# New places for the pieces of a hand-woven schedule: first layer's input, attention, delta layer

## The chip, the cores and the metric

The kernel runs on one core of one Trainium2 chip. The metric is the device time of one execution in microseconds (us), median of several runs. Of the kernel before, three runs are known: 3433.69, 3437.28 and 3441.73 us.

## The reference, cut to what matters

Two layers over x [2048, 1024]. Layer 0 is sparse attention on a latent, layer 1 a gated delta rule; after each comes a gated embedding. In the shape that the kernel uses:

```python
h = rms_norm(x, norm_w[0])
c_q, c_kv, k_idx, w_idx, z = split(h @ a_w_in)            # latents, each normed
score = sum_h relu(q_idx_h @ k_idx.T) * w_idx_h           # choose 256 keys per query
o = softmax(q_lat @ c_kv.T + bias, on the chosen keys) @ c_kv
x = x + ((o @ w_uv) * silu(z)) @ a_w_out;  x = x + sigmoid(...) * (p[0] @ ple_w_proj[0])

q, k, v = silu(causal_conv(h2 @ b_w_in));  beta, g = ...  # per head, in chunks
lower = strict(beta * k @ k.T * decay);   T = inverse(I + lower)
for each chunk:                                           # state S [128, 128] per head
    u = T @ (v - exp(g) * k @ S);  o = exp(g) * q @ S + (q @ k.T * decay) @ u
    S = S * decay_end + k_dec.T @ u
x = x + (rms_norm(o) * silu(z)) @ b_w_out;  x = x + sigmoid(...) * (p[1] @ ple_w_proj[1])
```

## The kernel before, in words

Every large matmul is done on values split into a high and a low part, as three matmuls (`mm3_step`, L90 to L92). TensorE therefore has most of the work, and the other engines prepare operands and take results out of PSUM.

The order of the work is written by hand. Each stage is a set of Python generators, the streams; a stream yields a position before each of its pieces, and `weave` always runs the piece with the smallest position (of equal ones, that of the stream named first). The order in which pieces are run is their order of priority on every engine and queue; the Tile framework then issues, at each engine, the first piece in that order that its own timing model has as ready. A position is a fraction of its stage (or a cost count), not a time.

The stages, in order of time:

- **Latents** (0 to 190 us). Four blocks of 512 rows. `latents(sb)` runs 22 steps of six matmuls: two column chunks of c_q (`ncq`), one of the index keys (`nki`), two of c_kv (`nkv`), with `at()` giving step n the position n / 23.7367. Beside it `enter(sb + 1)` loads the four 128-row tiles of the next block (`load_x`: a 512 KB load, a square with row sum on ScalarE into a scratch tile, a scale on VectorE), transposes and splits them into `hT`. The square of each chunk (`ncq..sq`, L265 to L268) and the scratch of `load_x` (`xsq`, L182) share the tag `sq`, which has two buffers. The sums over rows of the squares are matmuls with a column of ones (L276). `keep` writes the split input to HBM, two 512 KB writes at each of four steps.
- **Scores** (190 to 838 us). `index` (scores of the indexer), `topk` (bisection on VectorE and ScalarE), and `rest` (the gates z, keys, values, queries). `PLAN` gives index and topk of each block its window in units; 518 units is the whole.
- **Attention** (838 to 1414 us). `logits`, values (`turn` transposes the probabilities, `mult` multiplies with the values two turns later, at a place set by `MP`), loads, and at the start `proj_v`. `cost`, `C0` and `DELTA` say how far the values run behind the logits; `VS`, `VL`, `V0` place what comes before the first logits.
- **First mix**, then the **delta layer** (about 1840 to 3080 us), then the second mix. The delta layer has 18 passes j, each a weave. `project(j)` projects head j: tensors k, q, z, v in this order, two halves each, 32 steps of six 512-column matmuls (pieces `pB`). `within(j-1)` and `beside(j-1)` prepare the head before: k transposed (`pkt`), products (`pkk`, `pkq`), the inverse of a triangular matrix by 16 steps on VectorE (`tmp`, `inv`, L1639 and L1642), then through HBM (`iv_d`, `Uc`), a transpose `Tc`, and four rounds of small matmuls (`px`, `pd`) that fill `U`. `across(j-2)` carries the state over 8 chunks c of the head before that, each a chain of three pieces: `pks` (k and q times the state), `pu` (U times `y`), `po` (gives the new state). `gated` ends a head. `ahead` takes the place of project in the last two passes: first blocks of the output projection (`poe`).

Between the three pieces of a chunk stand small instructions of other engines: `pks` is followed by VectorE's `y` (L1749), `pu` by ScalarE's `uu` (L1757), `po` by VectorE's `state` (L1762). `raw_weights` splits the next tensor's weights: a copy on ScalarE (L1317) and a subtraction on VectorE (L1319, `wB`), each made to follow the last instruction that across has put on that engine.

```python
t0 = AC + c * AD                  # AC, AD = 0.0, 0.11
yield t0                          # pks, then y on VectorE
yield t0 + 0.035                  # pu, then uu on ScalarE
yield t0 + 0.07                   # po, then state on VectorE
```

## Time and profile before

| what | value |
|---|---|
| median of 3 runs | 3437.28 us |
| lowest, highest | 3433.69, 3441.73 us |
| the profiled execution, its time | 3443.02 us |
| its span, first to last instruction | 3441.3 us |
| mean granted TensorE clock in it | 0.982 |
| TensorE busy | 3304.1 us (96%) |
| VectorE, ScalarE, GpSimd busy | 2090.1, 1862.2, 950.1 us |

The profile counts TensorE's matmuls as pipelined, so a busy share is not a share of the peak. PEclk is the granted clock: 1.00 is 2.4 GHz and 0.5 is 1.2 GHz, and a stretch between has part of it at either level. In a timeline row the bracket gives how long the engine stood idle just before the instruction, and what ended the wait.

### The profile page before, as it was taken

To read this page: it belongs to the slowest core of one execution; us is meant where nothing else is said; L and a number is where in the kernel's file an instruction comes from. 1 tells how busy PE (TensorE), PEld (TensorE's weight loads), DVE (VectorE), ACT (ScalarE), POOL (GpSimd) and SP (SyncE) were. 2 spreads that over 40 slices of the span, in tenths; PEclk is the share of its full clock that TensorE was granted. 3 is DMA by queue.
4 is the path that set the end of the run, shared out by engine and by line. 5 is a ranking of instruction groups with operands and counts; after the bars stand their busy time and mean duration, and the time that the engine had idled before them with its cause. 6 is when DMAs were issued, how large, how long until landed. Compare 5 with 4: busy or idle time off the path is not lost.

```text
span 3441.3 us, 51940 instructions
## 1 busy us (share of the span) xinstructions
PE 3304.1 (96%) x18954; PEld 2773.9 (81%) x18954; DVE 2090.1 (61%) x4502; ACT 1862.2 (54%) x3255; POOL 950.1 (28%) x1620
## 2 busy tenths in 40 slices
PE   8999989998899999999999999999999999899999
PEld 6778877887799999888887788887788888678887
DVE  5347996773688888522134577677577677733222
ACT  5356958664677777533335465555565556434221
POOL 2022535246454445211100221231121232321100
PEclk9999999999999999999999999999999999999999
DMA  7532465443422222422222222222222222243212
GB/s 244 178 112 70 128 209 164 168 155 120 152 79 84 79 76 78 159 73 72 66 81 79 51 50 56 53 59 81 62 50 56 53 59 50 86 133 115 74 35 71
DMA packets 327596, 328.46 MB, mean 95 GB/s; under 512 B 69704, under 2 KB 273064, under 8 KB 323240
## 3 DMA queue, kind: packets, MB, share of 16 engines
q1 hardware_dynamic: 327336, 325.11, 31.1%
q8 instruction: 149, 2.44, 0.3%
q14 instruction: 111, 0.91, 0.1%
HBM read 221.24 MB, written 103.81 MB: 94 GB/s over the span
## 4 chain that ended last, share of the span: by engine, by line
PE 54%; DVE 11%; DMA 4%; POOL 2%; ACT 2%; issue 2%; SPq 0%; DVEq 0%; ACTq 0%; POOLq 0%
PE pgm L91 3%; PE pgm L92 3%; PE pgm L90 3%; PE pt L1024 3%; DVE tmp L1639 2%; PE pom L90 2%; PE pom L92 2%; PE pom L91 2%; PE pBv L1521 2%; PE po L1044 2%; PE pBv L1522 2%; PE po L1045 2%; PE lg L92 2%; PE pBv L1523 2%; PE lg L90 2%
## 5 line engine op out<-in xcount | busy, mean ns | idle before, releaser
L79 DVE TENSOR_TENSOR pl<-pt,ph 128x512 fp32r<-128x512 f32 (+1 forms) x288 | 187.7, 658 | 47.3 <-ACT ph L78 45.1
L78 ACT ACTIVATE ph<-pt 128x512 fp32r<-128x512 f32 (+1 forms) x288 | 159.8, 564 | 97.7 <-PE pt L1024 89.0
L1006 ACT ACTIVATE pr<-pr,nm,qscale 128x1024 f32<-128x1024 f32 (+2 forms) x192 | 189.5, 988 | 40.7 <-DVE nm L1003 39.7
L1247 DVE TENSOR_TENSOR gm<-ppm,gm 128x512 f32<-128x512 f32 x64 | 43.4, 690 | 244.3 <-ACT gm L1246 244.3
L423 DVE SCALAR_TENSOR_TENSOR score<-rl,wi,score 128x1024 f32<-128x1024 f32 (+7 forms) x154 | 170.0, 1127 | 35.2 <-ACT rl L415 34.3
L415 ACT ACTIVATE rl<-il 128x1024 f32<-128x1024 f32 (+7 forms) x176 | 142.7, 817 | 74.8 <-PE il L92 69.0
L1024 PE MATMUL pt<-ident,pr 128*128 128x128 f32 x1088 | 169.7, 276 | 8.2 <-ACT pr L1006 5.5
L90 PE MATMUL pom<-wo,ym 128*128 128x512 f32 x432 | 171.1, 396 | 1.9 <-DVE y L1056 1.1
L91 PE MATMUL pom<-wo,ym 128*128 128x512 f32 x432 | 169.4, 392 | 1.3 <-POOL wo L87 1.3
L91 PE MATMUL pgm<-wm,xh 128*128 128x512 f32 x432 | 168.9, 391 | 1.6 <-DVE wm L82 1.6
L729 DVE TENSOR_SCALAR_CACHE_REDUCE tkj<-score,t 128x1664 bf16<-128x1664 f32 (+3 forms) x91 | 121.9, 1353 | 79.0 <-POOL t L769 69.9
L90 PE MATMUL pgm<-wm,xh 128*128 128x512 f32 x432 | 169.0, 391 | 0.7 <-ACT gm L1246 0.6
L92 PE MATMUL pom<-wo,ym 128*128 128x512 f32 x432 | 169.2, 392 | 0.0
L92 PE MATMUL pgm<-wm,xl 128*128 128x512 f32 x432 | 169.0, 391 | 0.0
L1044 PE MATMUL po<-pl,kv 128*128 128x256 f32 x576 | 163.2, 283 | 1.7 <-DVE pl L79 1.6
L1045 PE MATMUL po<-ph,kv 128*128 128x256 f32 x576 | 162.3, 282 | 0.0
L1043 PE MATMUL po<-ph,kv 128*128 128x256 f32 x576 | 161.4, 280 | 0.8 <-ACT ph L78 0.6
L87 POOL TENSOR_TENSOR ym<-yr,ym 128x1024 fp32r<-128x1024 f32 x32 | 77.1, 2409 | 304.7 <-ACT ym L86 304.5
L1246 ACT ACTIVATE gm<-pgm,rm_r 128x512 f32<-128x512 f32 x64 | 42.9, 684 | 183.7 <-PE pgm L91 117.4
L727 ACT ACTIVATE tkj<-score,t 128x1920 bf16<-128x1920 f32 (+3 forms) x91 | 127.8, 1405 | 26.7 <-POOL t L769 13.6
L1752 ACT ACTIVATE qs<-pks,eg 128x128 f32<-128x128 f32 x120 | 44.0, 366 | 179.6 <-DVE y L1749 173.6
L90 PE MATMUL lg<-kv,q 128*128 128x512 f32 (+2 forms) x320 | 139.7, 437 | 0.7 <-DVE mx L997 0.7
(636 smaller groups left out, 10814.6 us busy)
## 6 DMA issues: line engine op xcount, KB each, us to landing
wBr<-in_b_w_in_dram SPq DMA_DIRECT2D x64, 512.0 KB
wr<-in_a_w_in_dram SPq DMA_DIRECT2D x74, 256.0 KB
hT_d<-hT SPq DMA_DIRECT2D x32, 512.0 KB
hz<-hT_d SPq DMA_DIRECT2D x16, 1024.0 KB
yr<-yT_d SPq DMA_DIRECT2D x32, 512.0 KB
x<-in_x_dram SPq DMA_DIRECT2D x16, 512.0 KB
zT_d<-z SPq DMA_DIRECT2D x32, 256.0 KB
k_d<-k SPq DMA_DIRECT2D x16, 512.0 KB
```

What stands on the lines that cost most here:

```text
L78: nc.scalar.activation(hi, src, AF.Copy)
L79: nc.vector.tensor_tensor(lo, src, f32(hi), ALU.subtract)
L90: nc.tensor.matmul(dst, ah, bh, start=first, stop=False)
L91: nc.tensor.matmul(dst, ah, bl, start=False, stop=False)
L92: nc.tensor.matmul(dst, al, bh, start=False, stop=last)
L415: nc.scalar.activation(rl[:, :s1 - s0], pl[:, :s1 - s0], AF.Relu)
L423: nc.vector.scalar_tensor_tensor(sc[:, s0:s1], rl[:, :s1 - s0], w, sc[:, s0:s1], ALU.mult, ALU.add)
L1006: nc.scalar.activation(pr[:, s0:s1], pr[:, s0:s1], AF.Exp, bias=nm, scale=sc, accum_out=den[:, i % 2, x:x + 1])
L1024: nc.tensor.transpose(pt[:, x * P:(x + 1) * P], probs[h, i][:, j * P:(j + 1) * P], ident)
L1043: nc.tensor.matmul(d, V[0][:, j], ph[:, c], start=st, stop=False)
L1044: nc.tensor.matmul(d, V[0][:, j], pl[:, c], start=False, stop=False)
L1045: nc.tensor.matmul(d, V[1][:, j], ph[:, c], start=False, stop=sp)
```

## The change

Positions and constants of the schedule are changed; no instruction is added, removed or changed. Lines without a sign are left out.

```diff
 # enter, latents: input of the first layer
-                yield (i / 8 + b / 4) * 0.989 + 0.0
+                yield (i / 8 + b / 4) * 0.9492 + 0.0812
-            if n in (6, 9, 12, 15):
-                keep(sb, (6, 9, 12, 15).index(n))
-            return n / 23.7367
+            if n in (2, 12, 14, 20):
+                keep(sb, (2, 12, 14, 20).index(n))
+            return n / 22.9662
 # proj_q
-                yield at + 0.013
+                yield at + 0.0181
 # attention
-    C0, DELTA = 1.5, 7.0
+    C0, DELTA = 1.269, 8.2959
-        cost = [4.0 * g + 3 + C0 for _, g in order]
+        cost = [3.7993 * g + 3 + C0 for _, g in order]
-            yield -VS + VL * 0.52
+            yield -VS + VL * 0.6127
-                yield begin[max(n - 2, 0)] + -0.02
+                yield begin[max(n - 2, 0)] + -1.0534
-    MP = 0.9
+    MP = 1.3291
-    VS, VL, V0, V1 = (40.0, 39.5, 39.0, 20)
-    PLAN = ({3: (0, 120), 2: (120, 256), 1: (300, 400), 0: (430, 470)}, {3: (122, 300), 2: (302, 415), 1: (417, 481), 0: (482, 530)}, 518)
+    VS, VL, V0, V1 = (40.0, 39.3825, 38.628, 20)
+    PLAN = ({3: (0, 120), 2: (120, 256), 1: (294, 400), 0: (418, 470)}, {3: (122, 300), 2: (302, 415), 1: (417, 483), 0: (482, 534)}, 518)
 # delta layer: places of within, beside, across, gated, ahead
-    VT, RA, RB = 0.36, 0.31, 0.0127
-    AC, AD, LV = 0.0, 0.11, 0.75
-    FX = 0.02
+    VT, RA, RB = 0.3282, 0.31, 0.0127
+    AC, AD, LV = 0.0, 0.11, 0.8179
+    FX = 0.0104
-                            if (sb, k) == (0, 0):
+                            if (sb, k) == (0, 3):
                                 made["raw"] = load_weights(n + 1)
-                            if (sb, k) == (1, 0):
+                            if (sb, k) == (0, 7):
                                 ready[n + 1] = raw_weights(n + 1, made.pop("raw"))
-            yield from by4(f"pkt{j}", transposes(kT), k_sink, 0.0)
+            yield from by4(f"pkt{j}", transposes(kT), k_sink, 0.0, 0.0297)
-            yield from by4(f"pkk{j}", prod(kT, kT), l_sink, 0.06)
+            yield from by4(f"pkk{j}", prod(kT, kT), l_sink, 0.06, 0.0105)
-            yield RA - 0.04
+            yield RA - 0.0591
-            yield LV - 0.02
+            yield LV - 0.0263
-                yield LV + 0.06 + p * 0.02
+                yield LV + 0.0609 + p * 0.02
-            yield LV + 0.14
+            yield LV + 0.123
-            yield LV + 0.2
+            yield LV + 0.2043
-            yield 0.12
+            yield 0.086
-                t0 = AC + c * AD
+                t0 = AC + c * AD + (c == NC - 1) * -0.0317
-                yield t0 + 0.035
+                yield t0 + 0.0265 + (0.0243 if c > 1 else 0)
-                yield t0 + 0.07
+                yield t0 + 0.0918 + {3: 0.0085, 7: 0.0071}.get(c, 0)
-            yield from by4(f"pot{j}", transposes(o), o_sink, at + 0.05)
+            yield from by4(f"pot{j}", transposes(o), o_sink, at + 0.0469)
-                at = 0.5 + x * 0.25 if part == 0 else x / n
+                at = 0.5842 + x * 0.25 if part == 0 else x / n
-                            yield at + (c * 4 + k // 2 + 1) / 9 * (0.25 if part == 0 else 1.0 / n)
+                            yield at + (c * 4 + k // 2 + 1) / 9 * (0.25 if part == 0 else 1.3319 / n)
```

## Rows read from the trace of the kernel before

**Rows 1.** The page's part 1: busy us, share of the span and instructions.
```profile
PE 3304.1 (96%) x18954; PEld 2773.9 (81%) x18954; DVE 2090.1 (61%) x4502; ACT 1862.2 (54%) x3255; POOL 950.1 (28%) x1620
```
**Rows 2.** Busy time by stage: stretch and length, engines, PEclk, DMA share, GB/s.
```profile
0.00:190.00 190.00, 170.28 (x840) 133.05 (x840) 85.98 (x135) 77.02 (x156) 32.43 (x52) 0.97 0.57 197
190.00:838.00 648.00, 608.69 (x2918) 502.20 (x2919) 492.00 (x704) 438.55 (x691) 258.75 (x554) 0.97 0.43 141
...
900.00:1400.00 500.00, 497.52 (x3639) 465.74 (x3637) 435.41 (x1385) 365.27 (x689) 230.07 (x282) 1.00 0.27 81
...
2480.00:2955.00 475.00, 466.44 (x3124) 388.77 (x3124) 335.50 (x762) 269.01 (x515) 114.59 (x261) 1.00 0.22 54
```
**Rows 3.** TensorE's waits by line, whole span: us in total, times, longest.
```profile
PE pu L1755 <- DVE y L1749: 17.4, 17, 5.4
...
PE ncq2ss L276 <- DVE ncq2sq L268: 3.3, 1, 3.3
PE ncq0ss L276 <- DVE ncq0sq L268: 2.6, 1, 2.6
...
PE px L1664 <- DVE Tc L1652: 2.6, 1, 2.6
```
**Rows 4.** Timelines of VectorE and TensorE in the latents: start, us, instruction, [idle].
```profile
125.15 0.69 DVE L267 TENSOR_TENSOR ncq2sq<-ncq2cr 128x512 f32<-128x512 f32 x1 [4.47 <-ACT xsq L182]
...
126.79 1.84 PE L276 MATMUL ncq2ss<-ones,ncq2sq 128*128 128x1 f32 x8 [3.34 <-DVE ncq2sq L268]
...
164.58 1.02 PE L276 MATMUL ncq3ss<-ones,ncq3sq 128*128 128x1 f32 x8
```
**Rows 5.** Busy time in four short stretches: engines, PEclk, DMA share, GB/s.
```profile
36.00:42.00 6.00, 4.94 (x20) 4.15 (x21) 1.70 (x3) 0.78 (x2) 1.65 (x2) 0.72 0.82 314
120.00:134.00 14.00, 10.10 (x44) 8.55 (x42) 6.82 (x11) 4.01 (x8) 1.95 (x1) 0.76 0.22 79
...
1938.00:1958.00 20.00, 20.00 (x123) 14.43 (x121) 4.31 (x6) 4.64 (x9) 1.15 (x5) 0.57 0.14 28
2672.00:2684.00 12.00, 12.00 (x144) 9.30 (x144) 4.88 (x9) 6.00 (x12) 3.12 (x7) 1.00 0.21 45
```
**Rows 6.** Timeline of TensorE, delta layer's second pass: the first px.
```profile
1937.59 0.66 PE L1664 MATMUL px<-Tc,LT 32*32 32x32 f32 x16 [2.57 <-DVE Tc L1652]
```
**Rows 7.** Timeline of TensorE, one later pass: its first pks, its px, the next pass.
```profile
2613.80 0.38 PE L1747 MATMUL pks<-state,kT 128*128 128x128 f32 x2
...
2672.84 1.09 PE L1664 MATMUL px<-Tc,LT 32*32 32x32 f32 x32
...
2683.18 0.38 PE L1747 MATMUL pks<-state,kT 128*128 128x128 f32 x2
```
**Rows 8.** Timelines of VectorE and TensorE in that pass, around chunk 6.
```profile
2660.54 1.23 DVE L1319 TENSOR_TENSOR wB<-wBr,wB 128x1024 fp32r<-128x1024 f32 x1
2661.68 1.01 DVE L1639 TENSOR_TENSOR tmp<-inv,blk 128x480 f32<-128x480 f32 x1
2662.59 0.35 DVE L1749 SCALAR_TENSOR_TENSOR y<-pks,neg,vt 128x128 f32<-128x128 f32 x1
...
2663.00 0.49 PE L1755 MATMUL pu<-y,U 128*128 128x128 f32 x2 [0.83 <-DVE y L1749]
```
**Rows 9.** Timeline of TensorE, pass without projection: po, then the next chunk's pks.
```profile
2964.15 0.39 PE L1761 MATMUL po<-uu,aq 128*128 128x128 f32 x2
2965.31 0.49 PE L1747 MATMUL pks<-state,kT 128*128 128x128 f32 x2 [0.77 <-DVE state L1762]
```
**Rows 10.** Timelines of VectorE and TensorE at the end of the scores.
```profile
823.20 0.85 DVE L806 TENSOR_TENSOR flags<-got,want 128x2 f32<-128x2 f32 x1
...
837.60 1.87 PE L477 MATMUL psq<-ones,qg 128*128 128x1 f32 x8 [3.06 <-DVE qg L509]
```
**Rows 11.** ScalarE by line, delta layer: count | busy us, mean ns | idle before.
```profile
L1468 ACT ACT_TABLE_LOAD x34 | 43.6, 1283 | 0.6
L1588 ACT ACT_TABLE_LOAD x16 | 20.5, 1283 | 1.2
```

## The prediction, made before the result was known

> **What bounds the kernel now.** I read the page's totals first, then busy time by stage, then TensorE's waits by line, and last the timelines around the longest of them. TensorE is busy for 3304.1 of 3441.3 us [rows 1], so no edit of places can give more than the other 137 us and what the clock gives back after a stall. The stages say where these are: the latents leave TensorE idle 20 of 190 us and the scores 39 of 648, while attention leaves 2.5 of 500 and the delta layer's second half 8.6 of 475 [rows 2]. In the waits the reader should see four that the moved pieces touch: `pu` on VectorE's `y`, 17.4 us, the row sums `ncq..ss` on their squares, 3.3 and 2.6 us, and `px` on `Tc`, 2.6 us [rows 3]. A stall costs twice: in the stretches that hold two of the latents' stalls the granted clock is 0.72 and 0.76, and in the 20 us after the `px` stall it is 0.57, though TensorE is busy through all of them; the same small matmuls of a later pass, with no stall ahead, run at 1.00 [rows 5].
>
> **The change part by part.** A place is a priority. What moves is which piece stands ahead of which, so I merge the streams' positions and count what changes sides.
>
> Latents. A step is 1/23.74 before and 1/22.97 after. `enter`'s piece that loads the last tile stood at 0.247, ahead of step 6; it now stands at 0.319, behind step 7. The second c_q chunk ends with step 7, so its square now comes ahead of that tile's square. Before, it came behind, and the two share a two-buffer scratch whose other buffer the first chunk holds: in the third block the square on VectorE waited 4.47 us for ScalarE's `xsq`, and the row sums stood 3.34 us for it [rows 4]. The fourth block has no next tile, and its row sums have no wait [rows 4]. The edit takes the cause away: 3.3 + 2.6 = 5.9 us of stall [rows 3], and of clock 6 × 0.28 + 14 × 0.24 = 5.1 us [rows 5], 11.0 in all. From the other side: the first of the four `keep` steps, 1 MB of writes, now stands ahead of the third tile's load, and if that tile becomes the late one the three waits come back, 0, or grow by one such stall each, +3 × 3.3 = 10 us. The third tile's square is now due six steps of six matmuls before the second chunk's, which is time enough, so I take 10 of the 11. The other `keep` steps only write to HBM, and the reader (the gates) starts after the stage; cover: the 190 us of the stage, and if a write were late, the next block's split would wait on `hT`, whose two buffers give it a whole block. `enter`'s last transposes stay ahead of step 21, so the next block does not start later.
>
> Scores. Two index windows start 6 and 12 units earlier and two topk windows end 2 and 4 later; a unit is 648/518 = 1.25 us. The last topk then ends 5 us later, at about 828 instead of 823.2, and the last queries end at 837.6 [rows 10]: hidden by some 9 us, and a loss of the excess if that cover went. Queue: the index pieces that move pass gates and value pieces, whose writes stand on SP; nothing else is passed. TensorE can win or lose a wait there, and the nearest row is 3.06 us [rows 10]. I take 0, with ±3. `proj_q`'s place moves inside its own stream, so nothing is passed.
>
> Attention. `VS`, `VL`, `V0` keep all four loads between the same pieces of `proj_v`, so 0. The values run 8.3 units behind the next group's start instead of 7, of some 18 units a group; TensorE idles 2.5 us in 500 [rows 2], so a gain ends there, and a lost wait is bounded by the same 3.06 us. The near bias is prepared about one unit earlier on GpSimd, with its loads on SP, while TensorE has other work. I take 0.
>
> Delta layer, second pass (the first with `within`). `LV` moves `px` from project's step 24 to step 27, and the matmuls behind it as far or somewhat less. Three steps are 18 matmuls; a step lasts about 69.4/32 = 2.2 us in a full pass [rows 7] and less in this one, so `px` comes 4 us or more later, and the 2.57 us that it waited for `Tc` [rows 6] are covered by projection. With the stall goes the low clock after it, 20 × 0.43 = 8.6 us [rows 5]. I take 2.6 + 8.6 = 11; the other end is 0, if the clock falls anyway.
>
> Delta layer, later passes. There `px` already stands 2672.84 - 2613.80 = 59 us into a pass of 69.4 [rows 7], behind where step 27 puts it, so `LV` gives nothing. The waits for `y` are 17.4 us in 17 times, one of them 5.4 in the pass without projection, which leaves 12.0 us for 16 [rows 3]. In a full pass it is chunk 6: `y` stood behind `wB` of 1.23 and a `tmp` of 1.01 us, and `pu` waited 0.83 [rows 8]. The weights' split moves up one matmul step in emission, but it is tied behind across's last instruction, and this is now chunk 5's `y` instead of its `state`, so `wB` goes some microseconds ahead and leaves the gap; the `tmp` stays. `pu` of chunk 6 keeps one step behind its `pks`. One of two obstacles goes: I take half, 6 of 12. The ends: 12 gained, or a loss that the next part prices. The 3-step later load of the weights waits on SP behind nothing new; the split needs it only four matmul steps on, and if it lands late ScalarE stands, with PSUM's two `pa` buffers as cover.
>
> The rest of the delta layer (`beside`, `gated`, the halves of `pkt` and `pkk`, `FX`, `ahead`) crosses a step here and there, beside a TensorE that has projection to do; 0, ±4 as in one such wait of 5.4 us.
>
> Sum: 10 + 11 + 6 = 27 us off the profiled execution's 3443.0, which gives 3416; that execution lies 5.7 us above the median, so against runs it is **3410 us**.
>
> A rule that speaks against the first term: the Trainium skill, Perfetto Trace Analysis (Identifying Performance Opportunities, Optimization Strategy), takes a gap that repeats on the busy engine as a possible sign of too few buffers. By that rule an order alone leaves the latents' stalls, and the sum is 17 us; the trace half agrees, since the wait is for a shared buffer [rows 4].
>
> **The rivals.**
>
> A, in part: one of the two stalls stays, because the third tile, behind 1 MB of writes, takes the last one's part, or because ScalarE or the clock keeps the second pass as it was. For it: both cures rest on one trace. Price: 10 or 11 of 27 us, so 3421.
>
> B, no change: the pieces come out where they stood. For it: `px` stands far behind its written place already [rows 7]. Against it: the latents' wait follows the order of two allocations. Time 3437.
>
> C, slower: the state's update is laid bare. Merging the places, `po` to the next `pks` has no projection step left at chunks 4 to 5 and 6 to 7, and one instead of two elsewhere. Where it is bare, `pks` waited 0.77 us for `state` [rows 9], and with half of a `wB` in flight on VectorE [rows 8] 0.77 + 0.62 = 1.4. Two places in 14 full passes are 28 waits, 39 us; less the 21 of the two stalls, 18 slower: 3455. It decides from 21/28 = 0.75 us a wait. Against it: a `pks` that is not ready lets projection pass.
>
> D, slower in another way: moved squares, exponentials and gates alternate more on ScalarE. There are 34 + 16 table loads at two lines alone, 1283 ns each [rows 11], in 16 heads. Two more a head between `pu` and `uu` are 16 × 2 × 1.28 = 41 us, less 27: 3451. The Trainium skill, ScalarE: Activation LUTs (Table sets: the hidden batching unit), says that each change to a function of another set costs a load, so order decides their number. ScalarE is busy 54% [rows 1], which speaks against.
>
> **How the numbers follow.** Forecast 0.55, A 0.17, B 0.14, C 0.10, D 0.04. A measurement of this kernel tells 0.2%, 7 us, from no change. Faster: forecast and A, 0.72. Same: B, 0.14. Slower: C and D, 0.14. The range's low end takes all gains, 11 + 11.2 + 12 and 3 + 2.5 + 4 from the parts held at 0, 44 us, with 3 for the spread of the runs: 3390. The high end takes in A and B with the upper bound of the runs known, 3442; C and D lie outside.
>
> **What would show it.** Right: no `xsq` ahead of `ncq..sq` and no wait of row sums above 1 us in the first 190 us; the second pass's `px` without a wait and PEclk at 1.00 behind it; fewer or shorter waits of `pu` for `y`. Wrong: waits of `pks` for `state` in every pass, more table loads, waits of row sums as before with a third tile's `xsq`, or a last topk behind the last queries.

## The result, and the profile after

| what | before | after |
|---|---|---|
| median of 6 runs each | 3439.74 us | 3396.76 us |
| lowest, highest | 3433.69, 3442.03 | 3390.05, 3406.71 |
| the profiled execution, its time | 3443.02 | 3399.54 |
| TensorE idle in the span | 137 us | 109 us |

The ratio is 0.9863, with an interval of 0.9844 to 0.9882: 43 us off medians, 43.9 us off the two profiled spans. The page's totals of the changed kernel, against [rows 1]:

```profile
PE 3288.3 (97%) x18954; PEld 2769.2 (82%) x18954; DVE 2113.0 (62%) x4502; ACT 1858.9 (55%) x3255; POOL 946.3 (28%) x1620
```

The counts of instructions are the same. TensorE is idle for 28 us less and busy for 15.8 us less. Summed over the span the latter is not the clock: its mean is 0.982 in both executions. A matmul behind a stall takes longer, as `pks` in two timelines below, 0.49 us with a wait and 0.38 without.

Where it went is read from the starts of five groups of matmuls: the last `pwi` ends the latents, the first `pv` the scores, the first `pom` the attention, `pBk` and the first `pom` behind it bound the delta layer. The tile views of the kernel before (count, ns, first and last start); the last row is of the stretch behind 2900 us:

```profile
L325 PE MATMUL pwi<-hT,widx_w x32: 388/392/398, 57.5 to 185.6; 128*16 128x512 f32 x32
...
L90 PE MATMUL pv<-wv,cv x32: 278/284/581, 841.1 to 855.3; 128*128 128x256 f32 x32
...
L90 PE MATMUL pom<-wo,ym x432: 387/390/629, 1415.6 to 3320.3; 128*128 128x512 f32 x144
...
L1521 PE MATMUL pBk<-hB,wB x256: 388/397/497, 1836.8 to 2907.4; 128*128 128x512 f32 x128
...
L90 PE MATMUL pom<-wo,ym x176: 387/390/629, 3078.8 to 3320.3; 128*128 128x512 f32 x176
```

And of the changed kernel:

```profile
L325 PE MATMUL pwi<-hT,widx_w x32: 388/396/397, 54.5 to 180.4; 128*16 128x512 f32 x32
...
L90 PE MATMUL pv<-wv,cv x32: 280/285/582, 831.0 to 845.8; 128*128 128x256 f32 x32
...
L90 PE MATMUL pom<-wo,ym x432: 388/389/497, 1402.2 to 3276.7; 128*128 128x512 f32 x144
...
L1521 PE MATMUL pBk<-hB,wB x256: 389/397/628, 1823.6 to 2865.9; 128*128 128x512 f32 x128
...
L90 PE MATMUL pom<-wo,ym x176: 389/389/497, 3036.2 to 3276.7; 128*128 128x512 f32 x176
```

The differences of the differences give the account: latents -5.2, scores -4.9, attention -3.3, first mix +0.2, delta layer -29.4, the rest -1.3 us. Inside the delta layer the second pass, from one pass's first `pBk` to the next, went from 66.3 to 54.3 us, and six full passes of the second half, which all do the same work, from 69.2 us each to 67.5. Those six, in the windows view (before, then after):

```profile
2476.50:2891.90 415.40, 408.04 (x2740) 340.26 (x2738) 292.31 (x660) 236.22 (x451) 100.45 (x229) 1.00 0.22 54
```

```profile
2445.40:2850.50 405.10, 405.10 (x2739) 341.90 (x2738) 300.29 (x660) 234.98 (x451) 98.07 (x228) 1.00 0.24 56
```

TensorE stood for 7.4 us of 415.4 before, and not at all after. The waits of before in these six passes:

```profile
PE pu L1755 <- DVE y L1749: 5.0, 6, 0.9
PE pot L1547 <- POOL vt L1790: 2.3, 6, 0.4
```

In the changed kernel's six passes TensorE has no wait at all. The window of the latents, against [rows 2]:

```profile
0.00:184.50 184.50, 169.30 (x840) 131.78 (x840) 84.61 (x134) 76.89 (x156) 31.55 (x52) 0.99 0.59 202
```

TensorE stands for 15 us instead of 20, in a stretch that is 5.5 us shorter. TensorE's waits by line, against [rows 3] (us in total, times, longest):

```profile
PE pz L90 <- DVE qi L79: 7.5, 2, 4.2
...
PE pv L90 <- ACT wv L86: 5.3, 1, 5.3
...
PE pu L1755 <- DVE y L1749: 3.9, 2, 3.4
PE ncq2pb L281 <- DVE ncq2r_r L163: 3.7, 1, 3.7
...
PE pks L1747 <- DVE state L1762: 2.7, 3, 1.6
...
PE ncq0ss L276 <- DVE ncq0sq L268: 1.0, 1, 1.0
```

`pu`'s waits for `y` fell from 17.4 us in 17 times to 3.9 in 2. Of the two row-sum waits, `ncq2ss`'s 3.3 us are gone and `ncq0ss`'s 2.6 are down to 1.0, but one `ncq2pb` of 3.7 us is new. Its place, in the timelines of ScalarE, VectorE and TensorE:

```profile
121.17 1.05 ACT L182 ACTIVATE xsq<-x 128x1024 bf16<-128x1024 f32 x1
...
122.54 0.24 ACT L161 ACTIVATE ncq2r_t<-ncq2ss,small 128x4 f32<-128x4 f32 x1
...
122.86 1.28 DVE L184 SCALAR_TENSOR_TENSOR x<-x,r_r,gain 128x1024 f32<-128x1024 f32 x1
...
124.38 1.09 PE L281 MATMUL ncq2pb<-ident,ncq2r_r 128*128 128x128 f32 x4 [3.75 <-DVE ncq2r_r L163]
```

The reader should see the last tile's square, `xsq`, once more. It no longer holds up the second chunk's square, as in [rows 4], but now stands on ScalarE ahead of the square root of the same chunk's row sums, and the same tile's scale, `x` on VectorE, stands ahead of the reciprocal (`ncq2r_r`) that `ncq2pb` waits for.

### The profile page after: what moved, and what is told of

The parts are those of the page before. It is cut to its first block, busy times and chain, and to the rows that moved or that the text cites. A ratio compares the mean times of both kernels' runs of the same rounds, so it can differ in the third digit from the quotient of the medians.

```text
span 3397.4 us, 51951 instructions
## 1 busy us (share of the span) xinstructions
PE 3288.3 (97%) x18954; PEld 2769.2 (82%) x18954; DVE 2113.0 (62%) x4502; ACT 1858.9 (55%) x3255; POOL 946.3 (28%) x1620
## 4 chain that ended last, share of the span: by engine, by line
PE 63%; DVE 4%; DMA 4%; ACT 3%; issue 1%; POOL 1%; SPq 0%; DVEq 0%; ACTq 0%; POOLq 0%
PE pgm L91 3%; PE pgm L90 3%; PE pgm L92 3%; PE pt L1024 3%; PE pom L91 2%; PE pom L90 2%; PE pom L92 2%; PE pBv L1521 2%; PE pBv L1523 2%; PE pBv L1522 2%; PE pBk L1521 2%; PE po L1044 2%; PE po L1045 2%; PE pBk L1523 2%; PE lg L92 2%; PE po L1043 2%
## 5 line engine op out<-in xcount | busy, mean ns | idle before, releaser
L727 ACT ACTIVATE tkj<-score,t 128x1920 bf16<-128x1920 f32 (+3 forms) x91 | 127.9, 1406 | 28.7 <-POOL t L769 17.4
L1024 PEld LDWEIGHTS pt<-ident,pr 128*128 128x128 f32 x1088 | 127.3, 142 | 14.2 <-ACT pr L1006 5.8
```

What stands on the lines that cost most here:

```text
L1024: nc.tensor.transpose(pt[:, x * P:(x + 1) * P], probs[h, i][:, j * P:(j + 1) * P], ident)
```

## The experiments

The change has seven separable parts: enter's places and the writes (latents), the scores' plan, attention's constants, and in the delta layer **LV**, the **split** of the next weights, **across** and the **rest** (`VT`, `FX`, `RA`'s piece, the halves of `pkt` and `pkk`, `beside`, `gated`, `ahead`). As a kernel's stages are read apart, one kernel tests parts of several stages. Each delta part was done alone, then taken back alone; two more kernels cut the rest in two, one joins the likely pair, and one tries a repair. Where an expectation gives 186.9 and 181.7 us for the latents, that is from the span's start to the last small transposes behind `pwi`; below the last `pwi` itself is used.

| kernel | median us | ratio to before, interval | latents end | scores | attention | delta | second pass | six passes, each |
|---|---|---|---|---|---|---|---|---|
| before | 3439.7 | 1 | 185.6 | 655.6 | 574.5 | 1242.0 | 66.3 | 69.2 |
| changed | 3396.8 | 0.9863, 0.9844 to 0.9882 | 180.4 | 650.7 | 571.2 | 1212.6 | 54.3 | 67.5 |
| LV alone | 3434.8 | 0.9980, 0.9965 to 0.9995 | 181.0 | 656.3 | 575.8 | 1232.3 | 55.4 | 70.4 |
| split alone | 3456.0 | 1.0045, 1.0027 to 1.0063 | 189.3 | 656.4 | 574.7 | 1245.0 | 61.3 | 70.2 |
| across alone | 3451.5 | 1.0032, 1.0014 to 1.0049 | 185.2 | 656.7 | 572.6 | 1251.3 | 58.9 | 70.9 |
| rest alone | 3468.1 | 1.0077, 1.0049 to 1.0106 | 182.6 | 651.4 | 577.4 | 1273.5 | 65.4 | 73.2 |
| LV taken back | 3414.3 | 0.9926, 0.9909 to 0.9943 | 176.4 | 651.6 | 572.2 | 1227.1 | 67.0 | 68.8 |
| split taken back | 3404.9 | 0.9897, 0.9880 to 0.9913 | 178.6 | 652.1 | 572.9 | 1216.3 | 54.3 | 68.1 |
| across taken back | 3437.5 | 0.9986, 0.9958 to 1.0015 | 181.6 | 651.3 | 573.3 | 1243.3 | 54.3 | 69.5 |
| rest taken back | 3431.5 | 0.9965, 0.9948 to 0.9982 | 179.5 | 650.8 | 571.4 | 1252.8 | 55.4 | 70.8 |
| across and rest | 3428.8 | 0.9953, 0.9938 to 0.9967 | 181.3 | 654.6 | 573.4 | 1227.7 | 66.7 | 67.9 |
| halves taken back | 3414.1 | 0.9923, 0.9896 to 0.9949 | 180.7 | 649.8 | 572.5 | 1224.2 | 54.7 | 69.9 |
| rest but halves taken back | 3416.1 | 0.9919, 0.9897 to 0.9941 | 182.1 | 650.3 | 573.6 | 1230.5 | 55.0 | 69.2 |
| changed, last tile later | 3396.7 | 0.9856, 0.9832 to 0.9881 | 176.7 | 649.9 | 571.1 | 1212.6 | 54.3 | 67.3 |

Each ratio is to runs of the kernel before that stand beside that kernel's; their medians are 3439.7 to 3445.9 us. Stage lengths are of each kernel's one profiled execution; stages that nothing was changed in differ by some 4 us, so smaller differences of one row are not argued from. Executions of one kernel can differ more: the ten with across taken back lie between 3416 us, at a mean granted clock of 0.984, and 3456 us, at 0.971. The profiled execution of rest taken back lies 10 us above its kernel's median, that of the rest but the halves taken back 7 us above, that of across and rest 7 us below, and their stage lengths share in that.

### One part at a time

**LV, and enter's places.**

```diff
-                yield (i / 8 + b / 4) * 0.989 + 0.0
+                yield (i / 8 + b / 4) * 0.9492 + 0.0812
...
-    AC, AD, LV = 0.0, 0.11, 0.75
+    AC, AD, LV = 0.0, 0.11, 0.8179
...
-            yield LV + 0.14
+            yield LV + 0.123
```

> The kernel before with two parts alone: the places of enter's pieces (first layer) and the LV group (delta layer). Latents, from the first matmul to the last pwi matmul 186.9 us before and 181.7 after. My theory (the order of the last tile's square against the second chunk's) says that the places do it alone: 180 to 183 us, no wait of ncq2sq, and the new wait of ncq2pb near 124 us comes with them. Rival (the writes' places do it): 186 to 188 us, with the waits of 3.3 and 2.6 us as before. Delta: my theory says that the second pass is 11 to 12 us shorter (66.3 to about 54.5) and that the steady passes keep their 69.2 us. Rival (LV gives the later passes too, since all of the inverse's pieces move with it): 67.2 us in the steady passes. Total by my theory 3437 - 5 - 12 = 3420 us, by the delta rival about 3405.

TensorE's waits of this kernel in the first 187 us hold no row sum of c_q, but the new wait of `ncq2pb`, 3.7 us once. So the places of enter's pieces alone take away `ncq2ss`'s wait, 3.3 us in all five kernels of the table with the old places, and bring the new one. `ncq0ss`'s wait is another matter. In across and rest, further below, the latents are those of before, and yet there it is

```profile
PE ncq0ss L276 <- DVE ncq0sq L268: 0.9, 1, 0.9
```

and 0.9 us in the rest alone too, against 2.6 to 3.1 in the other three with the old places. That its fall is the change's is therefore not shown, nor that all of the latents' 5.2 us are: they end at 181.3 to 185.6 us in the four kernels that leave them as before, and at 178.6 to 182.1 in the seven with enter's new places and the last tile as in the change, 3.1 us less between the means.

The second pass is 10.9 us shorter; the waits of `pu` for `y` stay (15.7 us in 17 times over the span), so LV gives the later passes nothing, as forecast. The six passes are even 1.2 us longer each in this execution.

**The split, and the writes.**

```diff
-            if n in (6, 9, 12, 15):
+            if n in (2, 12, 14, 20):
...
-                            if (sb, k) == (0, 0):
+                            if (sb, k) == (0, 3):
...
-                            if (sb, k) == (1, 0):
+                            if (sb, k) == (0, 7):
```

> The kernel before with two parts alone: the four keep steps with the step length (first layer) and the load and split of the next head's weights (delta layer). Latents: my theory says 186.9 us as before, with ncq2sq's wait for xsq; rival (the writes' places do it) 181 to 183. Delta: my theory says that the split ahead of chunk 6 shortens a steady pass by half to all of chunk 6's wait, 0.5 to 1.0 of 69.2 us, and that the second pass keeps its stall. Rival 1 (across's own places do it): 69.2 us kept. Rival 2 (the split alone is all of the gain): 67.2 us. Total by my theory 3437 - 10 = 3427 us.

```profile
PE pu L1755 <- DVE y L1749: 17.7, 17, 5.7
...
PE ncq2ss L276 <- DVE ncq2sq L268: 3.3, 1, 3.3
...
PE ncq0ss L276 <- DVE ncq0sq L268: 2.9, 1, 2.9
```

The latents keep both waits, as the theory says. The split fails it: over the span `pu` waits as often and as long as before, in the six passes 3.8 us instead of 5.0, and each pass is 1.0 us longer. Chunk 6 of one pass, in the timelines of VectorE and TensorE:

```profile
2665.63 1.22 DVE L1319 TENSOR_TENSOR wB<-wBr,wB 128x1024 fp32r<-128x1024 f32 x1
...
2669.03 1.03 DVE L1639 TENSOR_TENSOR tmp<-inv,blk 128x480 f32<-128x480 f32 x1
...
2670.38 0.49 PE L1755 MATMUL pu<-y,U 128*128 128x128 f32 x2 [0.62 <-DVE y L1749]
```

The split has gone by 2.2 us before this `tmp`, but the `tmp` alone still holds `y`: `pu` waits 0.62 us here and waited 0.83 before [rows 8].

**Across, and attention's constants.**

```diff
-                t0 = AC + c * AD
+                t0 = AC + c * AD + (c == NC - 1) * -0.0317
...
-                yield t0 + 0.035
+                yield t0 + 0.0265 + (0.0243 if c > 1 else 0)
...
-                yield t0 + 0.07
+                yield t0 + 0.0918 + {3: 0.0085, 7: 0.0071}.get(c, 0)
...
-    MP = 0.9
+    MP = 1.3291
```

> The kernel before with two parts alone: across's own places (delta layer) and all constants of the attention. Delta: my theory says that the split and across share the gain of the steady passes, so 0.5 to 1.0 of 69.2 us a pass here; rival 1 (all of it is across): 67.2 us; rival 2 (none of it): 69.2 us; a third, that across's places without the moved split cost a wait of y, 69.5 us or more. Attention, first value matmul to first output projection 574.5 before and 571.2 after: the constants give 3 us if they are the cause, 0 if the difference is the clock's or the neighbour stage's. Total by my theory 3437 - 10 - 3 = 3424 us.

Now the steady passes lose, as the third case has it, but not by a wait of `y`. TensorE's waits in this kernel's six passes (2474.1 to 2899.5 us):

```profile
PE pks L1747 <- DVE state L1762: 9.3, 18, 1.0
```

Three waits of `pks` for `state` a pass, 46 of them and 27.5 us over the span: this is rival C's mechanism, though in the pass below at chunks 3, 5 and 6, where C had 5 and 7. The longest of these three, in the timelines of VectorE and TensorE:

```profile
2660.45 1.22 DVE L1319 TENSOR_TENSOR wB<-wBr,wB 128x1024 fp32r<-128x1024 f32 x1
2661.58 0.99 DVE L1639 TENSOR_TENSOR tmp<-inv,blk 128x480 f32<-128x480 f32 x1
2662.48 0.35 DVE L1762 SCALAR_TENSOR_TENSOR state<-state,cd,po 128x128 f32<-128x128 f32 x1
...
2659.41 0.39 PE L1761 MATMUL po<-uu,aq 128*128 128x128 f32 x2
2662.88 0.49 PE L1747 MATMUL pks<-state,kT 128*128 128x128 f32 x2 [1.00 <-DVE state L1762]
```

`po` is done at 2659.8, but VectorE takes the split and a `tmp` first, 2.2 us together, so `state` comes 2.7 us behind `po`. In the changed kernel's pass the split has gone by when `po` comes:

```profile
2621.17 1.22 DVE L1319 TENSOR_TENSOR wB<-wBr,wB 128x1024 fp32r<-128x1024 f32 x1
...
2623.53 0.34 DVE L1762 SCALAR_TENSOR_TENSOR state<-state,cd,po 128x128 f32<-128x128 f32 x1
...
2622.86 0.39 PE L1761 MATMUL po<-uu,aq 128*128 128x128 f32 x2
2624.47 0.38 PE L1747 MATMUL pks<-state,kT 128*128 128x128 f32 x2
```

There `state` starts 0.3 us behind `po`'s end, and `pks` has no wait.

**The rest, and the scores' plan.**

```diff
-    VT, RA, RB = 0.36, 0.31, 0.0127
+    VT, RA, RB = 0.3282, 0.31, 0.0127
...
-            yield from by4(f"pkt{j}", transposes(kT), k_sink, 0.0)
+            yield from by4(f"pkt{j}", transposes(kT), k_sink, 0.0, 0.0297)
...
-            yield 0.12
+            yield 0.086
...
-    PLAN = ({3: (0, 120), 2: (120, 256), 1: (300, 400), 0: (430, 470)}, {3: (122, 300), 2: (302, 415), 1: (417, 481), 0: (482, 530)}, 518)
+    PLAN = ({3: (0, 120), 2: (120, 256), 1: (294, 400), 0: (418, 470)}, {3: (122, 300), 2: (302, 415), 1: (417, 483), 0: (482, 534)}, 518)
```

> The kernel before with the rest: in the delta layer VT, FX, the halves of pkt and pkk, beside, gated and ahead; in the scores PLAN and proj_q's place. Delta: my theory says that VT and the halves take away pot's wait for GpSimd's copy of vt, 0.6 us a steady pass (4.3 us in 7 times before), so about 68.6 of 69.2 us; rival 1: 69.2; rival 2 (the larger part of the 2 us is here): 68.0 or less. Scores 654.2 us before and 649.3 after: 649 to 651 if the plan does it, 654 if the latents' or the clock's share does it. Total by my theory 3437 - 8 - 5 = 3424 us.

The longest of all, 31.5 us more in the delta layer: none of the three cases held, and all had the wrong sign. The six passes in the windows view:

```profile
2478.50:2917.60 439.10, 429.70 (x2739) 350.15 (x2738) 293.67 (x660) 235.12 (x450) 98.42 (x228) 0.97 0.22 51
```

TensorE stands for 9.4 us (4.0 are `pks` for `state`, 3.1 `pot` for `vt`, 0.9 `px` for `Tc`), and the granted clock is 0.97 instead of 1.00, 1.2 GHz for about 6% of the 439 us, some 26 us at half speed, of which half is lost. By this estimate the clock is 2 us a pass of the 4 over the 69.2 of before.

The scores are 4.2 us shorter here, so the plan does that, or `proj_q`'s place, which moves with it in every kernel and was not tested apart. The five kernels of the table with the old plan have 654.6 to 656.7 us there, the nine with the new index windows 649.8 to 652.1.

### One part taken back

**LV back, and the last tile one piece later.**

```diff
-    AC, AD, LV = 0.0, 0.11, 0.8179
+    AC, AD, LV = 0.0, 0.11, 0.75
...
-                if i == 0 and b + 2 < 4:
+                if i == b and b + 2 < 4:
```

> The changed kernel with the LV group put back, and with one edit of its own in the first layer: the last tile is loaded one piece later (with the second piece of tile 1), so that its square stands behind the square root of the c_q row sums on ScalarE. Each part alone made a steady delta pass longer than the 69.2 us of before (68.6 to 69.5 with LV, 69.8 with the split, 70.4 with across, 71.5 with the rest, each with new waits of its own), all together 67.3. Theory: the parts of one pass cure each other's waits, across and the split above all, and LV only the second pass: second pass 62 to 66 us instead of 54.3, steady passes 67.3 to 68. Rival: every part is needed, 68.5 or more. Latents: end at 181.7 us after the change; theory: ncq2pb's wait of 3.7 us was for the square root behind the last tile's square, so it falls below 1.5 us and the stage ends 3 to 5 us earlier; rival: the wait moves on once more, to another row sum or to the last tile's transposes, and the stage ends where it did. Total by theory 3397 + 12 - 4 = 3405 us.

The waits go as the theory says, the lengths only in part. The second pass is back at 67.0 us, above the 62 to 66 expected. In the six passes TensorE stands for 0.35 us in all, but they take 68.8 us on average, which is in the rival's range: four of 67.2 to 67.8 and two of 71.7, with PEclk 0.98 over the six. So no new wait lengthens them; the two long passes go with the clock. The latents end at 176.4 us, 4.0 earlier, and the wait of `ncq2pb` is gone.

**The split back, and an earlier end of topk.**

```diff
-                            if (sb, k) == (0, 7):
+                            if (sb, k) == (1, 0):
...
-1: (417, 483), 0: (482, 534)}
+1: (417, 479), 0: (480, 524)}
```

> The changed kernel with the load and the split of the next head's weights put back, and with one edit of its own in the scores: the last two topk windows end at 479 and 524 instead of 483 and 534, so that the flags' count is read to the registers (4 us in which the engines stand at the end of the scores) while queries are still left. Theory: across needs the split in its new place, since the 1.22 us split stands otherwise between y and state of chunk 5, as with across alone: waits of pks for state in most passes, steady passes 69.5 to 70.5 us, total of the delta layer 30 to 40 us longer. Rival: the rest cures across too, 67.5 us. Scores: theory: the wait of pv for wv (5.3 us) falls to 1.7 or less, as before, and the stage is 3 to 5 us shorter than 649.1; rival: topk ahead of the queries costs TensorE as much elsewhere, 649. Total by theory 3397 + 35 - 4 = 3428 us.

The rival holds: across does not need the split moved, 68.1 us a pass and 3.7 us more in the delta layer. In the scores the edit gave nothing. Timelines of TensorE and VectorE at the end of the stage:

```profile
822.77 0.21 PE L665 MATMUL pf<-flags,ones 128*1 128x16 f32 x2
...
829.04 0.29 DVE L515 TENSOR_SCALAR psc<-psq 128x128 f32<-128x128 f32 x1 [4.18 <-DVEq L671]
```

The count of the flags (`pf`) is taken at 822.8 us, the changed kernel's at 825.5, but from the end of the latents that is 644.2 and 645.1 us: the edit moved it by 0.9 us only. VectorE stands in front of the branch (its queue, line 671) for 4.18 us, against 4.07 in the changed kernel and 4.34 before, with `psc` behind it. Whether a topk that ends clearly earlier can hide this is not tested.

**Across back, and the old end of topk.**

```diff
-                yield t0 + 0.0265 + (0.0243 if c > 1 else 0)
+                yield t0 + 0.035
...
-1: (417, 483), 0: (482, 534)}
+1: (417, 481), 0: (482, 530)}
```

> The changed kernel with across's own places put back, and with one edit in the scores: the last two topk windows end where they did before (481 and 530), the index windows stay as changed. Theory: without across's places the moved split stands ahead of y of chunk 5 or 6 again and pu waits, as before and with the split alone: 69 to 70 us a steady pass, 17 us of pu's waits for y. Rival: across is not needed, 67.5. Scores: if the end of topk decides, pv's wait for wv is between 5.3 and 1.7; if the index windows gave the 5 us, the stage stays at 649. Total by theory 3397 + 30 = 3427 us.

30.7 us longer in the delta layer, so all of its gain is lost, as expected; but not by the wait that I named. Over the delta layer `pu` waits 6.1 us in 4 times, while `pot` waits for `vt` 6.5 us in 14, `px` for `Tc` 4.3 in 13. TensorE stands there for 36.7 us instead of 24.3; the other 18.3 us are busy time, whose causes were not separated. The scores stay at 651.3 us with the old end of topk, so that end does not give the 5 us; the index windows, or `proj_q`'s place, are left.

**The rest back, and the old writes.**

```diff
-            yield 0.086
+            yield 0.12
...
-            if n in (2, 12, 14, 20):
+            if n in (6, 9, 12, 15):
```

> The changed kernel with the rest of the delta layer put back (VT, FX, the halves of pkt and pkk, beside, gated, ahead), and with the keep steps of before (6, 9, 12, 15) in the first layer. Theory: the rest alone gave the longest passes (71.5 us, state's waits and px's for Tc), so its parts only fit the new across; put back, pot waits 0.6 us a pass for vt again and the others stay cured: 67.8 to 68.3 us a steady pass. Rival 1: 69 or more, all four parts are one fit; rival 2: 67.3, the rest does nothing. Latents: the writes' places do nothing: end at 181.7 us, with ncq2pb's wait of 3.7 us; rival: they gave part of the 5 us, 183 to 187. Total by theory 3397 + 10 = 3407 us.

Rival 1: 70.8 us a pass and 40.2 us more in the delta layer, with 33 waits of `pks` for `state`, 18.8 us. So the change cannot spare the rest, the worst part alone. Whether the rest or across counts for more is open: TensorE stands in the delta layer for 44.1 us here and for 36.7 without across, but the medians, 3431.5 and 3437.5 us, are the other way round. The latents end at 179.5 us, so the writes' places are not what ends them earlier.

### The pair, the two cuts of the rest, and a repair

**Across and rest, split and LV as before.**

```diff
-            yield 0.12
+            yield 0.086
...
-                yield t0 + 0.035
+                yield t0 + 0.0265 + (0.0243 if c > 1 else 0)
```

> The kernel before with across's own places and the rest of the delta layer together, split and LV as before. Alone, across made the steady passes 70.4 us (from 69.2) and the rest 71.5; taken back from the change, across gives 68.6 to 69.4, the rest 70 to 71.6, the split 67.9, LV 67.3 to 67.8. Theory: these two are one fit, and together they give most of the steady passes' gain without the other two: 67.5 to 68.3 us, no wait of pu for y in chunk 6 and none of pot for vt, few waits of pks for state; the second pass keeps its 66 us. Total 3437 - 15 = 3422 us. Rival: the fit is of all four parts, and a pair alone has new waits of its own: 69 us or more, total 3437 or above.

67.9 us a pass. TensorE's only named wait in the six passes is

```profile
PE pks L1747 <- DVE state L1762: 1.5, 6, 0.3
```

and neither `pu` for `y` nor `pot` for `vt` is among them. The pair is the fit: alone the two cost 9.3 and 31.5 us of the delta layer, together they give 14.3. The ratios, which do not hang on one execution, agree: 1.0032 and 1.0077 alone, 0.9953 together.

**The halves back; the rest but the halves back.**

```diff
-            yield from by4(f"pkk{j}", prod(kT, kT), l_sink, 0.06, 0.0105)
+            yield from by4(f"pkk{j}", prod(kT, kT), l_sink, 0.06)
```

> The changed kernel with the places of the second halves of pkt and pkk put back. Theory: of the rest, these (the transposes and products ahead of across's first chunks) decide where the copies on ScalarE and the scaling on VectorE fall beside chunk 0 to 2, so without them the steady passes are 68.5 to 71 us with waits of pks for state or pot for vt. Rival: the halves do nothing, 67.3; then VT and beside are what across needs.

> The changed kernel with the rest of the delta layer put back except the halves: VT, FX, RA's piece, beside, gated and ahead as before. Theory, from the trace of the kernel without the whole rest, where the two convolutions of qT (1.52 us) run on VectorE from 38.6 us into the pass, just ahead of the state of a chunk whose po is at 38.7, while in the changed kernel they run from 36.8 with po at 37.6: VT or beside decides where these convolutions come, so the steady passes are 69 to 70 us with waits of pks for state and of pot for vt as there. Rival: the halves decide it, 67.3 here and 70 where they are put back.

Both lose, 69.9 and 69.2 us a pass, 11.6 and 17.9 us more in the delta layer (3414.1 and 3416.1 us by medians), so neither rival holds: across needs the halves and the others alike. Which of the others counts is open.

**The changed kernel with the last tile later.**

```diff
-                if i == 0 and b + 2 < 4:
+                if i == b and b + 2 < 4:
```

> The changed kernel with the last tile loaded one piece later, and nothing else. Where this edit stood beside LV's return, the latents ended 4.2 us earlier and ncq2pb's wait was gone. Theory: the other stages do not see it, 3397 - 4 = 3393 us, 0.9863 - 0.0012 = 0.985 of before. Rival: the next stage starts earlier and waits for the same transfers (il for rl, pz for hz), so the end stays at 3397.

The timelines of ScalarE and TensorE show the order turned round:

```profile
118.75 0.26 ACT L161 ACTIVATE ncq2r_t<-ncq2ss,small 128x4 f32<-128x4 f32 x1 [2.64 <-PE ncq2ss L276]
...
125.31 1.05 ACT L182 ACTIVATE xsq<-x 128x1024 bf16<-128x1024 f32 x1
...
120.97 0.60 PE L281 MATMUL ncq2pb<-ident,ncq2r_r 128*128 128x128 f32 x4
```

`ncq2pb` has no wait, and the latents end 3.7 us earlier; the two kernels with this edit, at 176.4 and 176.7 us, are clear of the other twelve. The scores and attention keep that, but the median is 3396.7 us against 3396.8, and the intervals of the two ratios overlap almost wholly. In the profiled execution the first mix and the stretch behind the delta layer, which the edit doesn't touch, are 3 us longer each, as in some of the other kernels. A gain of 4 us is neither shown nor excluded.

## Why the prediction was right, and where its terms were off

The forecast was 3410 us, the measured median 3396.8, inside the range and near its low end, which had been worked out as all gains at once. The direction held, and with it the cause in the second pass and that of one of the latents' two stalls. The other terms were mis-sized, to both sides: the latents gave 5 us less than forecast, the later passes, the scores and attention 20 us more. For those 20 us the prediction had no reason that held, so that they came is luck.

**Second pass: right in its place.** 11 us were forecast and 12.0 measured, with no wait of `px` and the clock at 1.00 behind it (window of the changed kernel, against 0.57 in [rows 5]):

```profile
1927.00:1947.00 20.00, 20.00 (x166) 16.53 (x166) 10.26 (x24) 10.44 (x19) 4.34 (x12) 1.00 0.15 29
```

That the clock's 8.6 us of this term fit is in part luck: the last section shows the same stall without a fall of the clock behind it.

**Latents: one cause right, term too large.** `ncq2ss`'s wait went with the order of two squares: the five kernels with the old places have it, the nine with the new ones do not. 10 us were forecast; 5.2 came in this pair of executions, and some 3 between the means of the kernels. (The clock's part of the forecast, 6 × 0.28 + 14 × 0.24, is 5.0 and not 5.1.) Two steps failed. I put `ncq0ss`'s 2.6 us down to the same order, but they fall to 0.9 in two kernels that leave the order as it was. And I merged the last tile's square against the second chunk's square on VectorE, and not against everything that ScalarE and VectorE have to do for that chunk: the square root and the reciprocal stand behind the tile's pieces, 3.7 us. By the rule of the Trainium skill, Perfetto Trace Analysis (Identifying Performance Opportunities), that such a gap can mean a want of buffers, the latents' stalls should have stayed. For `ncq2ss` the measurement decides against it, since the buffers are the same two and the 3.3 us are gone.

**Later passes: the largest miss.** 6 us forecast from the waits for `y`, and 0 for the rest of the delta layer; the delta layer gave 17.4 beside the second pass (29.4 - 12.0), of which 10.3 in the six passes of the windows above. The step "one of two obstacles goes", by which the moved split takes half of the waits for `y` away, is wrong: with the split alone it is out of the way in chunk 6, but the `tmp` is enough to hold `y`, and all 17 waits stayed. The step that held the rest at 0 because projection covers it is wrong too: across and the rest together take away the wait for `y`, 5.0 us in the six passes, and `pot`'s for `vt`, 2.3.

**Rival C was real.** Its mechanism came with across alone, 46 waits of 0.60 us, 27.5 us in all. A wait lay below the 0.75 us that I gave as the deciding price, but there were 46 and not 28, so their sum is above the 21 us that decide. The rest of the delta layer takes most of them away again: across and rest has 19, 8.6 us, the changed kernel 3, 2.7 us. **Rival D** fell. ScalarE by line in the delta layer has one table load more than [rows 11] at L1468, as many at L1588, and one fewer at L1525, where there were 3:

```profile
L1468 ACT ACT_TABLE_LOAD x35 | 44.9, 1283 | 0.6
...
L1525 ACT ACT_TABLE_LOAD x2 | 2.6, 1283 | 0.0
```

Over all lines they are 76 there, as before. B did not happen, and A not by its mechanism, though the latents' term came to half.

**Scores and attention: 0 forecast, 4.9 and 3.3 measured.** The nine kernels with the new index windows have the shorter scores, and `qi`'s wait for ScalarE's `va`, 4.1 to 4.3 us in the five with the old plan, is 0.3 at most in them. That wait alone is not the account, though: `pz`'s for `qi` rises from 4.2 to 7.5 us and `pv`'s for `wv` from 1.6 to 5.3. The whole stage, before and then after:

```profile
185.60:841.10 655.50, 613.92 (x2949) 506.45 (x2947) 495.16 (x710) 441.64 (x698) 259.59 (x558) 0.97 0.43 140
```

```profile
180.40:831.00 650.60, 610.62 (x2949) 503.94 (x2947) 498.06 (x710) 440.38 (x698) 260.48 (x557) 0.98 0.43 141
```

TensorE stands for 40.0 us instead of 41.6; the other 3.3 us are busy time, with a granted clock of 0.98 instead of 0.97. So the waits explain a third of the gain, and the rest is open. My step compared the end of topk with the end of the queries, and that cover indeed went, `pv` waits for `wv`; I had not asked what index passes. In attention the nine kernels with the new constants take 571.1 to 573.6 us; of the five others four take 574.5 to 577.4 and one 573.4. The constants give about 3 us, and hardly by a wait, since TensorE stands there for 17.5 us before and 17.2 after; by what is open.

## What to carry to other kernels

Where several streams are merged by written places, a part of a change has no value of its own. The four delta parts, alone, add up to +34 us (-9.7 + 3.0 + 9.3 + 31.5), and together they gave -29.4. These lengths are of single executions, but the ratios agree: the first four kernels behind the changed one in the table hold the whole change between them and add up to 1.3% slower, the change is 1.4% faster. So judge such a change by merging all streams in full, each engine's queue beside TensorE's, and don't call a part harmless because projection stands beside it; and when a piece is moved past one reader of a late engine, look for the next instruction of the same chunk on every engine it touches.

## What the hardware showed that was not expected

The clock that a stall costs is not fixed. With across alone, the second pass has the same wait of `px` for `Tc` as before, 2.6 us, but the window behind it runs at full clock:

```profile
1939.00:1959.00 20.00, 20.00 (x173) 15.64 (x170) 5.64 (x9) 8.10 (x16) 1.72 (x7) 1.00 0.15 27
```

Before it was 0.57 [rows 5]. The pass took 58.9 us here and 66.3 before, and 54.3 without the wait. So, as an estimate from these lengths, of the 12 us that the change gained in this pass 4.6 are the stall and what goes with it, and 7.4 a fall of the clock that the same stall does not always bring. The kernels that keep this wait gave 58.9, 61.3, 65.4, 66.3, 66.7 and 67.0 us for the pass.

Nor was the clock's part kept in these two executions. Over the whole delta layer, before and after:

```profile
1836.80:3078.80 1242.00, 1195.18 (x7655) 982.17 (x7655) 824.75 (x1846) 677.87 (x1265) 294.32 (x624) 0.98 0.24 62
```

```profile
1823.60:3036.20 1212.60, 1188.29 (x7655) 984.53 (x7655) 841.29 (x1846) 674.60 (x1265) 290.19 (x624) 0.97 0.26 64
```

TensorE's idle time fell from 46.8 to 24.3 us, but the mean clock is a little lower, since it fell in other passes instead, some of them with no stall ahead: four full passes of the first half are 67.3 us twice and 68.3 twice, and in the six of the second half one of 68.8 stands among five of 67.2 to 67.3. That one holds a fall of the clock, though TensorE has no wait in any of the six:

```profile
2706.00:2716.00 10.00, 10.00 (x103) 7.82 (x103) 2.06 (x4) 3.81 (x8) 0.19 (x1) 0.83 0.36 36
```

Counted over the layer, the gain is stalls and the longer matmuls behind them, not clock.
